# Summing six conditioning columns of layer 1 behind layer 0's last projections

## The chip, the cores and the metric

The kernel runs on one core of one Trainium2 chip. The metric is device time in microseconds (us), the median of three executions. TensorE (PE), VectorE (DVE), ScalarE (ACT) and GpSimd (POOL) compute; SyncE (SP) issues nearly all DMAs, one after the other in the order in which the code emits them.

## The reference

A trunk of two layers over 512 tokens of 1024 features, all in float32. A conditioning vector `c` gives six vectors of 1024 per layer, that is twelve columns of 512; each column is a product of the 1024 values of silu(c) with a 1024 x 512 block of `ada_w`.

```python
c_act = jax.nn.silu(c)
for i in range(DEPTH):                                   # DEPTH = 2
    mod = c_act @ ada_w[i] + ada_b[i]                    # 6 * 1024 = 12 columns of 512
    sh1, sc1, g1, sh2, sc2, g2 = jnp.split(mod[:, None, :], 6, axis=-1)
    h = x * (1 + sc1) + sh1
    y = neighbourhood_mixer(...) if i == 0 else gqa_mixer(...)
    x = layer_norm(DEEPNORM_ALPHA * x + (1 + g1) * y, ...)
    h = x * (1 + sc2) + sh2
    y = hierarchical_moe(h, ...)                         # 32 experts, each 6 MB of weights
    x = layer_norm(DEEPNORM_ALPHA * x + (1 + g2) * y, ...)
```

## The kernel before

**Stages.** Layer 0 has a neighbourhood attention (`mixer0`), then the output projection with the router (the loop over `sums`, `turnX`, `logits`), then the mixture of experts (`moe`, 16 pairs of experts). Layer 1 is the same with another attention.

**The loop around the change.** `flow` (line 155) writes out the order of layer 0's attention by hand, for PE, DVE and SP. It has 32 steps n, one for each pair of heads i = n // 4 and query block b = n % 4. A step emits: the scores of step n+1, some projection matmuls (`fill`), `close` of the finished pair of heads, the transposes of the probabilities (`turn`), a DVE share of one conditioning column (`adav`), `aside`, more projection matmuls, `adap` where the table `ADAP` names the step, and the weighted sum of the values (`weigh`). The projections of `STREAM` supply `fill`; they read the normalised input `hTH`, `hTL` and run out by step 27. Then `end` (the function `done`) closes the pool `ht0` that holds the input, opens in its memory four tiles `wh` for the split of the output weights `wo`, and from step 28 on `aside` calls `step`, which splits one quarter of `wo` into two parts.

**Conditioning columns.** Layer 0's columns 0 to 3 come first. Seven columns (`ADAV`) are summed on DVE. The others (`ADAP`, line 47) are summed on PE in `adap` (line 689): a column has eight products of a 128 x 32 slice of `Z` with a 128 x 512 slice of the weights, in four column groups of the array, so two of eight go to each group; the sum stands in a PSUM tile `pt` and DVE adds it to `mod[l]` (line 699). Layer 1's columns 6 to 11 are taken in pairs at steps 15, 19 and 23, its column 3 alone at step 26.

**Weights.** `plan` lists all loads in the order of their use, and `W` (line 242) issues them on SP as slots of `wp` (five tiles of 1 MB), and later of other pools, come free. A column needs two loads of 1 MB. SP holds strictly to its order: a load whose slot is still being read holds all that are behind it. The last loads of the attention are column (1, 3) and the four of `wo`; the third and fourth of `wo` take the two slots that column (1, 3) leaves.

**After the loop.** `close(7)` scales the last heads, `flush` adds the last DVE column. Then `layer` opens on the same side of the memory the pools `hr` and `wk`: `g1` (two `row` matmuls into `pw`, line 934, and line 935), and `oH`, `oL` (lines 1019, 1020), the split of the attention's output, which the first output projection (`pw<-w,oH`) reads. Tiles of a new pool wait for the last reader of the tiles whose memory they take.

Of the kernel before, what the change touches and what calls it, by code (L numbers as in the profile page):

```python
# [8 lines left out]
F32 = mybir.dt.float32  # L9
# [4 lines left out]
OP = mybir.AluOpType  # L14
# [3 lines left out]
P = 128  # L18
# [7 lines left out]
F = 512  # L26
# [17 lines left out]
QPOST = 2  # L44
NWQ = 4
ADAV = [(0, 6), (0, 7), (0, 8), (0, 9), (1, 0), (1, 1), (1, 2)]
ADAP = {4: [(0, 4), (0, 5)], 8: [(0, 10), (0, 11)], 12: [(1, 4), (1, 5)], 15: [(1, 6), (1, 7)], 19: [(1, 8), (1, 9)],
        23: [(1, 10), (1, 11)], 26: [(1, 3)]}
STREAM = [("qk", 1, 0)] + [("qk", n, i) for i in (1, 2) for n in range(2)] + [("vq", 0)] \
    + [("qk", n, i) for i in (3, 4, 5, 6) for n in range(2)] + [("vq", 1)] + [("qk", n, 7) for n in range(2)]  # L50
RATE = (18, 15)
# [10 lines left out]
def bcast(ap, shape):  # L62
    return ap.to_broadcast(shape)


class Trunk:
    def __init__(self, ctx, tc, a, out, dbg=None):
        self.ctx, self.tc, self.nc, self.a, self.out = ctx, tc, tc.nc, a, out
        self.dbg = dbg or {}
        self.wl = []  # L70
        self.qfree = NWQ
        self.wi = 0
        self.wt = {}
        self.wpos = {}
        self.extra, self.free, self.owed, self.nh = [], [0] * NWB, 0, None

# [5 lines left out]
    def plan(self):  # L82
        a, wl = self.a, self.wl

        def add(key, ap, dst=None):
            self.wpos[key] = len(wl)
            wl.append((key, ap, dst))

        def ada(l, *js):
            for j in js:  # L90
                for h in range(2):
                    add(("ada", l, j, h), a["ada"][l, j, h])

        def direct(key, ap, dst):
            add(key, ap, dst)

        def xs(c0, c1):
            for t in range(NT):
                direct(("x", t, c0), a["x"][t][:, c0:c1], self.X[t][:, c0:c1])

        def aq(j, c):
            add(("aq", j, c), a["adaq"][j, c])

        for n, t in self.early:
            direct(n, a[n], t)
        for g in range(4):
            aq(g // 2, g % 2)
            aq(2 + g // 2, g % 2)
            if g == 0:
                for l in range(DEPTH):  # L110
                    direct(("adab", l), a["adab"][l], self.mod[l][0:NR])
                xs(0, 256)
                add(("v", 0, 0), a["wv"][0])
                add(("qk", 0, 0), a["wqk"][0, 0])
            elif g == 1:
                xs(256, 512)
            elif g == 2:
                xs(512, 1024)
                add(("v", 0, 1), a["wv"][1])
        for n, t in self.late:  # L120
            direct(n, bcast(a[n], [P, 36]) if n[:2] == "rb" else a[n], t)
        def ask(z):
            if z[0] == "ada":
                add(z, a["ada"][z[1], z[2], z[3]])
            elif z[0] == "qk":
                add(z, a["wqk"][z[1], z[2]])
            else:
                add(z, a["wvq"][z[1]])

        none = lambda *n: None  # L130
        self.flow(ask, lambda z, ahead: chunk_dry(z, ahead), none, none, none, none, lambda z, h, k: k or ask(("ada", *z, h)),
                  lambda pair: [ask(("ada", *z, h)) for z in pair for h in range(2)], none, none)
        for l in range(DEPTH):
            if l:
                for c in range(2):
                    add(("kv", c), a["wkv1"][c])
                for c in range(4):
                    add(("q1", c), a["wq1"][c])
            for h in range(2):
                for kh in range(2):  # L140
                    add(("wo", l, h, kh), a["wo"][l, h, kh])
            for h in range(2):
                for kh in range(2):
                    add(("wl", l, h, kh), None)
            for j in range(E // 2):
                for n in range(2):
                    for kh in range(2):
                        for i in range(2):
                            add(("gu", l, 2 * j + i, n, kh), a["gu"][l, 2 * j + i, n, kh])
                for fh in range(2):  # L150
                    for i in range(2):
                        add(("dn", l, 2 * j + i, fh), a["dn"][l, 2 * j + i, fh])
            self.wend = getattr(self, "wend", []) + [len(wl)]

    def flow(self, split, chunk, scores, turn, weigh, close, adav, adap, aside, end):


        todo, made, ready = list(STREAM), [0], set()

        def ahead():  # L160
            if todo:
                z = todo.pop(0)
                split(z)
                ready.add(z)

        def stream():
            for z in STREAM:
                if z not in ready:
                    ahead()
                for _ in chunk(z, ahead):  # L170
                    made[0] += 1
                    yield
            while True:
                made[0] += 1
                yield

        it, due, n = stream(), {}, 0
        for z in STREAM:
            n += 48 if z[0] == "vq" else 24
            due[z] = n  # L180

        def fill(n):
            for _ in range(n):
                next(it)

        def need(z):
            fill(max(0, due[z] - made[0]))

        need(("qk", 1, 0))
        scores(0)  # L190
        for n in range(32):
            i, b = n // 4, n % 4
            if n + 1 < 32:
                if b == 3:
                    need(("qk", 1, i + 1))
                scores(n + 1)
            rate = RATE[n >= 12]
            fill(rate // 2)
            if b == 0 and i:
                close(i - 1)  # L200
            turn(n)
            if i < len(ADAV):
                for k in range(2):
                    adav(ADAV[i], b // 2, 2 * (b % 2) + k)
            aside(n)
            fill(rate - rate // 2)
            if n in ADAP:
                adap(ADAP[n])
            if n == 16:
                need(("vq", 0))  # L210
            if n == 24:
                need(("vq", 1))
            weigh(n)
            if n == 27:
                end()
# [137 lines left out]
    def ada_cols(self, pool, mod, dst, js, tag):  # L353
# [4 lines left out]
        for n, j, one in js:  # L358
            nc.vector.tensor_scalar(dst[:, n].rearrange("p (j i) -> p j i", j=2),
                                    pc[:, :, j:j + 2].rearrange("p i j -> p j i"), one, None, op0=OP.add)  # L360

    def row(self, ps, l, j):
        return self.mm(ps, bcast(self.indc[:, j:j + 1], [P, P]), self.mod[l], True, True)

# [64 lines left out]
    def mixer0(self, oT, right):  # L429
        tc = self.tc  # L430
        with tc.tile_pool(reuse_waits="tile", name="v0", bufs=1) as vp:
            self.qk_pool = vp
            V = vp.tile([P, NT, D], F32, name="V")
            V6 = vp.tile([P, NT - 1, D], F32, name="V6")
            ht = tc.tile_pool(reuse_waits="tile", name="ht0", bufs=1, side="right")
            hp = ht.__enter__()
            hH = hp.tile([P, KD, S], F32R, name="hTH")
            hL = hp.tile([P, KD, S], F32R, name="hTL")
            self.qpool = hp
            wo = []  # L440
            with tc.manual_schedule(engines={mybir.EngineType.PE, mybir.EngineType.DVE}), \
                    tc.tile_pool(reuse_waits="tile", name="n0p", bufs=2, space=PSUM) as pp:
                q0 = self.values(vp, pp, hp, hH, hL, V, V6)
                with tc.tile_pool(reuse_waits="tile", name="n0", bufs=1) as pool:
                    def done():
                        ht.__exit__(None, None, None)
                        wo.extend(self.split_wo(0, right("wh", 4)))

                    self.neighbours(pool, pp, hp, hH, hL, V, V6, oT, q0, done, lambda: wo[1]())
        return wo  # L450

    def split_wo(self, l, pool):
# [133 lines left out]
    def neighbours(self, pool, pp, hp, hH, hL, V, V6, oT, q0, done, step):  # L586
        nc, a = self.nc, self.a
# [41 lines left out]
        bias, pr, pt, po, rz = {}, {}, {}, {}, {}  # L629
# [40 lines left out]
        def close(i):  # L670
            self.scaled(pool, pp, oT[i // 4][:, i % 4, :].rearrange("p (b q) -> p b q", b=4), po[i], rz[i])
# [17 lines left out]
        def adap(pair):  # L689
# [8 lines left out]
                                tile_position=(0, r))  # L698
            nc.vector.tensor_tensor(self.mod[l], self.mod[l], ps, op=OP.add)

        def aside(n):
            i, b = n // 4, n % 4
            if b == 1 and i and i % 2 == 0:
# [6 lines left out]
            if n >= 28:  # L710
                step()

        self.flow(split, chunk, scores, turn, weigh, close, adav, adap, aside, done)
        close(7)
        self.accs, self.accl = [(j, accs.pop((l, j))) for l, j in ADAV[6:]], 1
        self.flush(pp)

# [919 lines left out]
```

## Time and profile before

| | |
|---|---|
| median of 3 runs | 1659.25 us (1657.05 to 1659.85) |
| the profiled execution | 1659.12 us; span from first to last instruction 1657.4 us |
| busy: PE, DVE, ACT, POOL | 95%, 42%, 26%, 10% of the span |
| layer 0's attention loop | 71 to 288 us |
| layer 0's output projection and router | 292 to 372 us |
| layer 0's experts | 377 to 850 us |
| DMA | 493 MB, 298 GB/s over the span, 419 GB/s beside the experts |

Times in the views are microseconds from the span's start. "Idle before" names what ended an engine's wait; SPq is SP's sequencer; PEclk is the granted clock of TensorE, 1.00 for 2.4 GHz and 0.50 for 1.2 GHz. A float32 product is two matmul instructions, so a column's eight products are 16 instructions.

### The profile page before, as it was taken

The numbers are of one execution on the slowest core, as the hardware profiler recorded it, in microseconds if no ns is written. First come the engines' busy times: TensorE is split into PE (matmuls) and PEld (weight loads), VectorE is DVE, ScalarE is ACT, GpSimd is POOL, SyncE is SP. The second block draws the span as 40 slices with busy tenths as digits, with TensorE's granted clock in tenths as the row PEclk, the third lists the DMA queues.
The fourth block names the chain that finished last, engine by engine and source line by source line (L and its number), as shares of the span: only waits on it lengthen the run. The fifth ranks groups of instructions, "written<-read, shape, count | busy, mean of one in ns | idle before, by whom it ended". The sixth has DMA issues, their size and how long they took to land. (4 is left out here: it accounts for less than half of the span.)

```text
span 1657.4 us, 21364 instructions
## 1 busy us (share of the span) xinstructions
PE 1569.4 (95%) x8490; PEld 903.9 (55%) x8490; DVE 700.5 (42%) x1605; ACT 437.8 (26%) x934; POOL 162.7 (10%) x99
## 2 busy tenths in 40 slices
PE   7999997989999999999989989998999999999995
PEld 5676664673544545455448866766444545445442
DVE  3434545574332322323256865666432322323235
ACT  2343335231110111111134475453111111101112
POOL 2322212010000000000013250011000000000001
PEclk9999997999999999999989999999999999999997
DMA  9586972358999999999942000035999999999971
GB/s 335 185 314 261 353 290 105 152 203 328 413 419 420 419 419 420 419 419 420 419 154 83 27 1 26 1 127 206 418 412 420 420 419 420 419 420 419 419 326 52
DMA packets 76198, 493.17 MB, mean 298 GB/s; under 512 B 9876, under 2 KB 11284, under 8 KB 18876
## 3 DMA queue, kind: packets, MB, share of 16 engines
q1 hardware_dynamic: 72636, 485.44, 72.1%
q10 hardware_dynamic: 3456, 6.29, 1.2%
q8 instruction: 69, 1.13, 0.3%
q14 instruction: 37, 0.30, 0.1%
HBM read 489.61 MB, written 2.10 MB: 297 GB/s over the span
## 5 line engine op out<-in xcount | busy, mean ns | idle before, releaser
L300 PE MATMUL gu<-w,xT 128*64 128x512 f32 x2048 | 445.1, 592 | 0.0
L300 PEld LDWEIGHTS gu<-w,xT 128*64 128x64 f32 x2048 | 146.8, 137 | 291.8 <-issue 285.5
L300 PE MATMUL pd<-w,hx 128*64 128x512 f32 x1024 | 226.8, 595 | 0.0
L1391 DVE TENSOR_TENSOR h<-h,gu 128x512 f32<-128x512 f32 x32 | 22.0, 688 | 367.5 <-PE gu L300 367.5
L300 PEld LDWEIGHTS pd<-w,hx 128*64 128x64 f32 x1024 | 70.7, 137 | 137.9 <-issue 134.3
L300 PE MATMUL gc<-OH,zH 128*128 128x256 f32 x480 | 121.8, 291 | 2.4 <-DVE OH L1276 2.4
L300 PE MATMUL gc<-OH,zL 128*128 128x256 f32 x480 | 118.9, 285 | 0.0
L300 PE MATMUL gc<-YH,OT 128*128 128x512 f32 x244 | 104.1, 427 | 1.0 <-DVE X L1358 1.0
L1358 DVE TENSOR_TENSOR X<-X,gc 128x512 f32<-128x512 f32 x128 | 87.3, 687 | 39.5 <-PE gc L300 39.5
L313 POOL TENSOR_TENSOR wl<-w,wh 128x1024 fp32r<-128x1024 f32 x19 | 46.1, 2431 | 559.5 <-DMA kk<-in_gain 494.4
L300 PEld LDWEIGHTS gc<-OH,zH 128*128 128x128 f32 x480 | 92.7, 193 | 14.7 <-issue 11.4
L300 PE MATMUL gc<-YL,OT 128*128 128x512 f32 x244 | 96.3, 395 | 0.0
L300 PEld LDWEIGHTS gc<-OH,zL 128*128 128x128 f32 x480 | 92.9, 193 | 0.0
L300 PE MATMUL pw<-w,oH 128*128 128x512 f32 x256 | 87.5, 413 | 0.4 <-DVE g L935 0.4
L1294 ACT ACTIVATE xT<-gc,A 128x256 f32<-128x256 f32 x60 | 33.8, 566 | 174.1 <-PE gc L300 174.1
L1414 ACT ACTIVATE YH<-h 128x512 fp32r<-128x512 f32 x32 | 20.2, 630 | 219.8 <-DVE h L1413 219.8
L300 PE MATMUL pj<-wh,hTH 128*128 128x256 f32 (+1 forms) x272 | 70.9, 303 | 6.7 <-ACT wh L312 2.8
L300 PE MATMUL pj<-wl,hTH 128*128 128x256 f32 (+1 forms) x272 | 68.0, 292 | 0.0
L300 PE MATMUL pj<-wh,hTL 128*128 128x256 f32 (+1 forms) x272 | 65.3, 292 | 1.4 <-DVE hTL L427 1.4
L300 PEld LDWEIGHTS gc<-YH,OT 128*128 128x128 f32 x244 | 45.8, 188 | 37.2 <-DVE X L1358 15.7
L1390 ACT ACTIVATE h<-gu 128x512 f32<-128x512 f32 x32 | 19.1, 597 | 174.3 <-PE gu L300 174.3
L1292 DVE TENSOR_SCALAR xT<-gc,A 128x256 f32<-128x256 f32 x60 | 32.5, 544 | 76.7 <-ACT xT L1294 76.3
(345 smaller groups left out, 2362.9 us busy)
## 6 DMA issues: line engine op xcount, KB each, us to landing
w<-in_gu SPq DMA_DIRECT2D x256, 1024.0 KB, 13.9
w<-in_dn SPq DMA_DIRECT2D x128, 1024.0 KB, 13.2
w<-in_ada SPq DMA_DIRECT2D x40, 1024.0 KB, 7.6
wq<-in_wqk SPq DMA_DIRECT2D x16, 512.0 KB, 3.6
w<-in_wo SPq DMA_DIRECT2D x8, 1024.0 KB, 4.8
w<-in_adaq SPq DMA_DIRECT2D x6, 1024.0 KB, 11.5
bias<-in_nab ACTq DMA_DIRECT2D x24, 256.0 KB, 4.4
w<-in_wq SPq DMA_DIRECT2D x4, 1024.0 KB, 4.8
```

The costliest lines, as they stand in the source:

```text
L300: return self.nc.tensor.matmul(out, l, r, start=start, stop=stop, **kw)
L313: (eng or nc.gpsimd).tensor_tensor(lo, src, h.bitcast(F32), op=OP.subtract)
L1292: nc.vector.tensor_scalar(xT[q][:, k, :], ps, s, b, op0=OP.mult, op1=OP.add)
L1294: nc.scalar.activation(xT[q][:, k, :], ps, AF.Identity, scale=s, bias=b)
L1358: nc.vector.tensor_tensor(X[t][:, c], X[t][:, c], ps, op=OP.add)
L1390: nc.scalar.activation(h, gu[0], AF.Silu)
L1391: nc.vector.tensor_tensor(h, h, gu[1], op=OP.mult)
L1414: nc.scalar.activation(YH[j][:, c], y, AF.Copy)
```

## The change

Layer 1's columns 6 to 11 leave the table `ADAP` and the list of `plan`. A list `qa` of 24 loads of 512 KB takes their place, four for a column. `done` opens a pool `aq0` of four such tiles (2 MB, one column) right behind the `wh` tiles, in memory that the closed pool `ht0` held, and issues the first four loads behind `wo`'s. `adaq` sums one column: eight products that read the four tiles in turn, one DVE add, and then the next four loads, each of which waits on SP until its tile has been read. It is called at steps 28 to 31, between `aside` and `weigh`, and twice behind `close(7)`. The pool is closed before the pools `hr` and `wk` are opened, which so take its memory.

```diff
-ADAP = {4: [(0, 4), (0, 5)], 8: [(0, 10), (0, 11)], 12: [(1, 4), (1, 5)], 15: [(1, 6), (1, 7)], 19: [(1, 8), (1, 9)],
-        23: [(1, 10), (1, 11)], 26: [(1, 3)]}
+ADAP = {4: [(0, 4), (0, 5)], 8: [(0, 10), (0, 11)], 12: [(1, 4), (1, 5)], 26: [(1, 3)]}
+ADAQ = [(1, j) for j in (8, 9, 6, 7, 10, 11)]
...
+        self.qt, self.qa = [], [(l, j, h, x) for l, j in ADAQ for h in range(2) for x in range(2)]
...
             if n in ADAP:
                 adap(ADAP[n])
+            if n > 27:
+                adaq()
...
+    def ada_tiles(self):
+
+        while self.qfree and self.qa:
+            l, j, h, x = z = self.qa.pop(0)
+            t = self.qpool.tile([P, 1024], F32, name="wa", bufs=NWQ)
+            self.nc.sync.dma_start(t, self.a["ada"][l, j, h][:, 1024 * x:1024 * x + 1024])
+            self.qt.append((z, t.rearrange("p (k n) -> p k n", k=2)))
+            self.qfree -= 1
...
                     def done():
                         ht.__exit__(None, None, None)
                         wo.extend(self.split_wo(0, right("wh", 4)))
-
-                    self.neighbours(pool, pp, hp, hH, hL, V, V6, oT, q0, done, lambda: wo[1]())
+                        self.qpool = qp.enter_context(tc.tile_pool(reuse_waits="tile", name="aq0", bufs=1, side="right"))
+                        self.ada_tiles()
+
+                    with ExitStack() as qp:
+                        self.neighbours(pool, pp, hp, hH, hL, V, V6, oT, q0, done, lambda: wo[1]())
...
+        def adaq():
+            if self.qt:
+                l, j = self.qt[0][0][:2]
+                ps = pp.tile([P, F], F32, name="pt")
+                for n in range(4):
+                    _, w = self.qt.pop(0)
+                    self.qfree += 1
+                    for k in range(2):
+                        kk = 2 * n + k
+                        r = 32 * (kk % 4)
+                        self.mm(ps[r:r + 32], self.Z[:, kk, 12 - j:44 - j], w[:, k, :], kk < 4, kk > 3, tile_position=(0, r))
+                nc.vector.tensor_tensor(self.mod[l], self.mod[l], ps, op=OP.add)
+                self.ada_tiles()
...
         close(7)
+        adaq()
+        adaq()
```

## Rows read from the trace of the kernel before

**Rows 1.** Page, part 1: busy time, share of the span, instructions.

```profile
PE 1569.4 (95%) x8490; PEld 903.9 (55%) x8490; DVE 700.5 (42%) x1605; ACT 437.8 (26%) x934; POOL 162.7 (10%) x99
```

**Rows 2.** Table by stretch: busy of each engine, granted clock, DMA share, GB/s.

```profile
core 0: us, PE busy (x) PEld busy (x) DVE busy (x) ACT busy (x) POOL busy (x), PEclk, DMA share, GB/s
150.00:200.00 50.00, 48.56 (x305) 31.26 (x304) 26.68 (x54) 19.25 (x45) 11.95 (x5) 1.00 0.90 352
250.00:300.00 50.00, 40.58 (x209) 24.56 (x208) 24.53 (x54) 22.02 (x54) 11.04 (x8) 0.76 0.41 153
500.00:800.00 300.00, 300.00 (x1544) 145.25 (x1542) 85.55 (x164) 41.38 (x81) 0.00 (x0) 1.00 1.01 419
```

**Rows 3.** Waits, 380 to 845: PE's for DMAs; us in total, times, longest.

```profile
PEld gu L300 <- DMA w<-in_dn: 2.0, 7, 0.3
PEld pd L300 <- DMA w<-in_gu: 0.9, 3, 0.3
```

**Rows 4.** Timeline of PE: the summed columns at steps 15, 19, 23 and 26.

```profile
177.80 2.78 PE L300 MATMUL pt<-w,Z 128*32 128x512 f32 x24
182.02 1.06 PE L300 MATMUL pt<-w,Z 128*32 128x512 f32 x8 [1.44 <-DMA w<-in_ada]
...
205.89 3.64 PE L300 MATMUL pt<-w,Z 128*32 128x512 f32 x32
...
237.98 3.64 PE L300 MATMUL pt<-w,Z 128*32 128x512 f32 x32
...
263.01 3.64 PE L300 MATMUL pt<-w,Z 128*32 128x512 f32 x16
```

**Rows 5.** Timeline of PE, 229 to 295: waits and the way into the output projection.

```profile
231.74 0.80 PE L300 MATMUL pj<-hTH,wh 128*128 128x512 f32 x1 [2.46 <-ACT V L479]
...
274.06 0.63 PE L303 MATMUL pt<-c_ident,rze 128*128 128x128 f32 x4 [2.27 <-DVE rze L886]
...
276.19 1.12 PE L300 MATMUL po<-pts,V 128*64 128x128 f32 x8 [1.07 <-DVE w L893]
...
288.02 1.12 PE L300 MATMUL po<-pts,V 128*64 128x128 f32 x8 [0.75 <-ACT pts L658]
...
290.19 1.92 PE L300 MATMUL pt<-dacc,Zo 128*32 128x512 f32 x2
292.04 2.19 PE L300 MATMUL pw<-mod,c_indc 128*128 128x512 f32 x4
294.68 0.73 PE L300 MATMUL pw<-w,oH 128*128 128x512 f32 x2 [0.45 <-DVE g L935]
```

**Rows 6.** Timeline of SP, and time to landing of each: `wo`'s third and fourth load.

```profile
265.00 0.33 SPq L272 DMA_DIRECT2D w<-in_wo  x1
...
DMA to landing us min/median/max: 4.8/4.8/4.8
...
266.71 0.33 SPq L272 DMA_DIRECT2D w<-in_wo  x1
...
DMA to landing us min/median/max: 6.8/6.8/6.8
```

**Rows 7.** Page, part 6: loads of 512 KB; count, size, median us to landing.

```profile
wq<-in_wqk SPq DMA_DIRECT2D x16, 512.0 KB, 3.6
```

**Rows 8.** Table by stretch, cut where the granted clock changes; columns as in rows 2.

```profile
231.05:237.90 6.85, 6.16 (x16) 4.57 (x16) 2.00 (x4) 2.36 (x6) 0.00 (x0) 0.50 0.44 157
...
261.80:268.60 6.80, 6.80 (x35) 2.96 (x34) 0.69 (x1) 3.51 (x8) 0.00 (x0) 0.50 0.36 125
268.60:275.40 6.80, 3.14 (x26) 1.99 (x24) 5.10 (x15) 4.91 (x14) 2.69 (x2) 1.00 0.49 184
275.40:292.50 17.10, 13.25 (x59) 7.42 (x60) 11.45 (x21) 8.19 (x20) 8.35 (x6) 0.50 0.14 42
```

**Rows 9.** Timelines of ACT and DVE: split of the attention's output, and `g1`.

```profile
265.49 1.14 ACT L1019 ACTIVATE oH<-w 128x512 fp32r<-128x512 f32 x2
...
293.96 1.27 DVE L935 TENSOR_SCALAR g<-pw 128x512 f32<-128x512 f32 x2
```

**Rows 10.** DVE's adds of a column sum: count, ns min/median/max, first and last start.

```profile
L699 DVE TENSOR_TENSOR mod<-mod,pt x7: 687/690/690, 103.1 to 266.7; 128x512 f32<-128x512 f32 x7
```

More of the change, by code (lines that the diff above doesn't have):

```diff
@@ L131, in plan @@
         self.flow(ask, lambda z, ahead: chunk_dry(z, ahead), none, none, none, none, lambda z, h, k: k or ask(("ada", *z, h)),
-                  lambda pair: [ask(("ada", *z, h)) for z in pair for h in range(2)], none, none)
+                  lambda pair: [ask(("ada", *z, h)) for z in pair for h in range(2)], none, none, none)
         for l in range(DEPTH):
@@ L153, in plan, with flow @@
             self.wend = getattr(self, "wend", []) + [len(wl)]
-    def flow(self, split, chunk, scores, turn, weigh, close, adav, adap, aside, end):
+    def flow(self, split, chunk, scores, turn, weigh, close, adav, adap, adaq, aside, end):
         todo, made, ready = list(STREAM), [0], set()
@@ L711, in aside @@
                 step()
-        self.flow(split, chunk, scores, turn, weigh, close, adav, adap, aside, done)
+        self.flow(split, chunk, scores, turn, weigh, close, adav, adap, adaq, aside, done)
         close(7)
+        adaq()
+        adaq()
+        assert not self.qa and not self.qt
         self.accs, self.accl = [(j, accs.pop((l, j))) for l, j in ADAV[6:]], 1
```

## The prediction

> **What bounds the kernel now.** I read the busy shares first: PE works 95% of the span, everything else less than half [rows 1]. Such a share is a mean over stages, so the table by stretch comes next [rows 2]. In the attention loop PE is at 48.6 of 50 us; from 250 to 300 it falls to 40.6 of 50 at a mean granted clock of 0.76; beside the experts it is at 300 of 300 with the DMAs at 419 GB/s. Both PE and DMA are full there, so the waits decide which of them leads: from 380 to 845 PE waits for weights ten times, 2.9 us in all, never over 0.3 us [rows 3]. The experts thus run at PE's pace, and a microsecond won or lost before 377 is one at the end. The change lies wholly before that. The question is therefore when the first matmul of the output projection starts, which is 294.68 [rows 5].
>
> I cut the time before it at a point both kernels have: T, the end of column (1, 3)'s sum at step 26, 263.01 + 3.64 = 266.65 [rows 4]. What is removed lies before T, what is added behind it.
>
> **Before T: three pairs of columns go.** They take 2.78 + 1.06 us with a wait of 1.44 us for their weights between them at step 15, then 3.64 us at step 19 and 3.64 us at step 23 [rows 4]: 12.56 us from start to end, some 0.2 us less as neighbouring matmuls overlap, so 12.4 us. PE is full in this stretch [rows 2] and in order, so the gain is taken whole: T moves to about 254.3. Nothing hides it and nothing else was hidden by it; the matmuls of `fill` and `turn` around them stay. Three DVE adds of 0.69 us [rows 10] also go, on an engine that waits there for PE. The loads behind them on SP (the projections' weights, `wo`'s first two) only come earlier. The bound below for this part is 12.4 - 3 us, if one more stretch at half clock falls into it, the one above 12.4 + 3 us: the wait of 2.46 us at step 22 to 23 (a PSUM buffer that ACT must empty) is followed by 6.85 us at clock 0.50 with 6.16 us of matmul work [rows 5, 8]. If the clock stays at 1.00 there, half of that work's time, 3.1 us, is won as well. The wait itself stays, so I take nothing.
>
> **Behind T: what PE must do.** Six columns are 96 matmul instructions. Sixteen take 3.64 us at clock 0.50, and 32 as long at 1.00 [rows 4, 8], so a column costs 1.8 us at full and 3.6 us at half clock. Steps 28 to 31 have room for some of it: they run from about 274 to 288 in a chain from engine to engine, PE waits 0.75 to 2.27 us in each (six waits from 268.7 on, of which three stand in [rows 5]), and the clock is at 0.50 with 13.25 of 17.10 us busy [rows 8]. With PE's work alone the six columns would nearly fit.
>
> **Behind T: what the loads must do.** They are the term that decides. SP keeps its order, so the new loads stand behind `wo`. The third and fourth loads of `wo` wait for the two slots of column (1, 3), at T - 1.65 and T + 0.06, and the fourth lands 6.8 us after its issue [rows 4, 6], T + 6.9. The first four tiles are issued right behind it and move in its wake: 2.10 MB at 419 GB/s [rows 2] are 5.0 us, T + 11.9. PE has come to step 28's call by about T + 7 (in the kernel before the transposes of that step end at 276.19 - 1.07 = 275.12, T + 8.5, behind a wait of 2.27 us for DVE [rows 5], of which I let 1.5 go, since DVE's early share of the split of the attention's output moves behind the columns), so it waits for tiles. The last tile's four instructions end the first column at T + 12.6.
>
> Every further column needs its own 2.10 MB, and there are only four tiles: a tile is asked for again when its products are through. Lower bound: the transfer never pauses, 5.0 us for a column. Upper bound: nothing overlaps; the first tile's load takes 3.6 us to land [rows 7], three more follow at 1.25 us each (512 KB at 419 GB/s), the last is read in 0.5 to 0.9 us, 8 us in all. Between them lies the nearest row, two loads issued 1.7 us apart: `wo`'s third lands 4.8 us after its issue and the fourth 3.7 us later [rows 6], where 1 MB at 419 GB/s would take 2.5 us. That is 283 GB/s with two in flight; with two to four in flight I take the middle, some 360 GB/s, so 5.8 us a column. Between two columns at steps 28 to 31 PE does `weigh`, scores and transposes in about 2 us at full clock (3.4 us at half, [rows 5]); their loads run meanwhile, so this lies beside the transfer. Five columns more: 29.0 us, and the last ends at T + 41.6.
>
> What queues behind these waits: PE is in order, so `weigh` of steps 28 to 31 and the scores behind it stand still with the column; DVE's add for it (0.69 us) stands ahead of the scores' maxima of the next step; on SP the first expert weights stand behind all 24 loads. The last of these is no cost: expert weights are wanted at 377, and SP is through by about T + 36.
>
> Then the way into the output projection. In the kernel before it is 294.68 - 290.19 = 4.5 us from `flush` to the first matmul, mostly at half clock [rows 5]. In the changed kernel one more DVE add stands in it, and the tiles of `hr` and `wk` (`oH` among them) take the memory of the four tiles, so the first splits of the attention's output, done at 265.49 in the kernel before [rows 9], must wait for the last column's products; against that, PE may be at full clock. Bounds 2.5 and 4.5 us, I take 3.5.
>
> **The sum.** New start of the output projection: T + 12.6 + 29.0 + 3.5 = T + 45.1. Before: 294.68 - 266.65 = T + 28.0. Loss 17.1 us, gain 12.4 us: slower by 4.7 us. The profiled execution took 1659.12 us (span 1657.4), 0.1 us under the median of 1659.25, so the forecast is 1664 us. With the bounds of the unknown terms: 5.0 us a column and 2.5 us at the end give T + 40.1, a change of -0.3 us, 1659; 7 us a column and 4.5 us at the end give T + 52.1, +11.7 us, 1671.
>
> **The rivals.** A measurement of this kernel can tell about 0.2%, 3.3 us, from no change.
>
> Same: the four tiles keep the DMA engines full, 5.0 to 5.3 us a column. For it: four loads in flight reach 419 GB/s beside the experts [rows 2]. Against it: there the loads don't wait for one another's readers. Result 1659 to 1661.
>
> Faster: the clock. Removing work shifts the wait at step 23 against the clock's changes, and columns on PE fill the idle steps. If the stretch at 231 keeps clock 1.00 (3.1 us) and the columns also come at 5.0 to 5.3 us, the result is 1659 - 3.1 to 4, about 1655.5. For it: in the steps before, waits of 1.44 us left the clock at 1.00 [rows 2, 4]. Against it: the wait of 2.46 us stays. It decides from the point where a column costs under 5.3 us, since above that the loss behind T eats the clock's gain.
>
> Clearly slower: PE stands at half clock through the six columns. Then `weigh`, scores and transposes (3.4 us) and a column's products (3.6 us) no longer fit beside the transfer, 7 us a column: 1671. For it: waits of about 1.1 us between short matmuls kept the clock at 0.50 from 275.40 to 292.50 [rows 5, 8], and the columns' waits for tiles will be as long. Against it: at 7 us PE would be busy without a gap, and the dense work at 261.80 to 268.60 ended with a return to 1.00 [rows 8].
>
> The Trainium skill ("TensorE: Matmul & The Clock Gate", section "Loop structure matters more than you think") names a wait for a DMA ahead of every group of matmuls as the loop that lets TensorE go cold, and that is how the moved columns are built: by that rule it is this last rival, 1671. The trace shows the fall to half clock behind one wait of 2.46 us and not behind one of 1.44 us [rows 4, 5, 8].
>
> **How the numbers follow.** Forecast (5.4 to 6.5 us a column) 0.42, same 0.28, faster 0.15, clearly slower 0.15. The forecast's own range reaches from 1661.5 to 1668, so a part of it (0.05) lies within 0.2%, and a part of the same rival (0.02) falls below it. Faster 0.17, same 0.31, slower 0.52. The range 1655 to 1671 takes in the faster and the clearly slower case at their centres and leaves out 0.2 beyond.
>
> **What the profile would show.** T at about 254. Twenty-four loads of 512 KB on SP, landing over some 36 us from about 255. Matmuls `pt<-w,Z` in six groups from about 262 to 296, with waits for `w<-in_ada` ahead of each; their spacing is the term to read: 5.0 is the same rival, 5.8 the forecast, 7 at clock 0.50 the slow one. First matmul of the output projection at about 299, and everything behind it shifted as a block. I am wrong if the spacing is 5 us or less, if T falls by much more or less than 12.4 us, or if the experts' pace changes.

## The result and the profile after

The changed kernel takes 1674.78 us (median of 4 runs, 1673.18 to 1675.61) against 1658.74 us of the kernel before on the same chip: a ratio of 1.0101, 95% interval 1.0088 to 1.0113. It is slower by 16 us, where 5 were forecast, and lies above the range. The profiled execution took 1675.56 us with a span of 1673.8, against 1659.12 and 1657.4 before.

The busy shares of the page hardly moved (they answer to [rows 1]):

```profile
PE 1579.0 (94%) x8490; PEld 905.7 (54%) x8490; DVE 695.9 (42%) x1608; ACT 437.5 (26%) x934; POOL 161.0 (10%) x99
```

The timeline of PE shows the whole loss. The columns are start, length, engine, line, operation, tiles, count, and in brackets the wait ahead of it with its releaser. The first line is column (1, 3), whose end is T; `wa` are the four new tiles; the last two lines answer to the last two of [rows 5].

```profile
250.08 3.64 PE L303 MATMUL pt<-w,Z 128*32 128x512 f32 x16
...
262.96 3.07 PE L303 MATMUL pt<-wa,Z 128*32 128x512 f32 x12
266.24 1.05 PE L303 MATMUL pt<-wa,Z 128*32 128x512 f32 x4 [0.21 <-DMA wa<-in_ada]
...
273.22 1.05 PE L303 MATMUL pt<-wa,Z 128*32 128x512 f32 x4 [1.42 <-DMA wa<-in_ada]
274.45 1.05 PE L303 MATMUL pt<-wa,Z 128*32 128x512 f32 x4 [0.18 <-DMA wa<-in_ada]
...
281.05 1.05 PE L303 MATMUL pt<-wa,Z 128*32 128x512 f32 x4 [0.22 <-DMA wa<-in_ada]
...
288.41 1.05 PE L303 MATMUL pt<-wa,Z 128*32 128x512 f32 x4 [0.19 <-DMA wa<-in_ada]
...
296.29 1.05 PE L303 MATMUL pt<-wa,Z 128*32 128x512 f32 x4 [0.21 <-DMA wa<-in_ada]
...
304.23 0.62 PE L303 MATMUL pt<-wa,Z 128*32 128x512 f32 x2 [2.19 <-DMA wa<-in_ada]
...
304.68 0.60 PE L303 MATMUL pt<-wa,Z 128*32 128x512 f32 x2
...
305.22 3.64 PE L303 MATMUL pw<-mod,c_indc 128*128 128x512 f32 x4
...
309.15 0.70 PE L303 MATMUL pw<-w,oH 128*128 128x512 f32 x2 [0.29 <-DVE g L967]
```

T is 250.08 + 3.64 = 253.72, 12.9 us earlier than before. The six columns end at 267.29, 275.5, 282.1, 289.46, 297.34 and 305.28: the first at T + 13.6, then five in 38.0 us, **7.6 us a column**. The output projection starts at 309.15 = T + 55.4, 14.5 us later than before. The first matmul of layer 0's experts goes from 376.74 to 392.19 (15.5 later) and layer 1's from 1154.81 to 1171.50 (16.7 later); the span grows by 16.4. So most of the loss is there when the output projection starts.

What PE waits for between 250 and 312 (total us, times, longest), and the table by stretch from the first column to the end of the last, and the 3.4 us behind it (columns as in [rows 2]):

```profile
PE pt L303 <- DMA wa<-in_ada: 11.2, 14, 2.2
PEld pt L303 <- DMA wa<-in_ada: 24.5, 17, 3.1
...
264.20:305.20 41.00, 28.48 (x152) 7.05 (x146) 10.37 (x23) 8.84 (x22) 7.48 (x6) 1.00 0.88 297
305.20:308.60 3.40, 3.40 (x7) 1.18 (x4) 3.27 (x6) 0.00 (x0) 0.00 (x0) 0.50 1.01 426
```

PE is at full clock for 41 us and idle for 12.5 of them. The DMA engines are at work for 0.88 of the time and move 297 GB/s (the first expert weights, from 297.76 on, included), where beside the experts they are at work all the time and move 419 [rows 2]. They are thus idle for only an eighth of the time; the rest of the missing rate is that they move less while at work. The loads themselves, from the instructions of line 370 and from SP's timeline (they answer to [rows 6, 7]):

```profile
L370 SPq DMA_DIRECT2D wa<-in_ada x24: 327/328/1154, 254.2 to 297.4; - x24
...
DMA to landing us min/median/max: 3.8/6.2/10.6
...
264.66 33.05 SPq L370 DMA_DIRECT2D wa<-in_ada  x20
...
297.76 0.42 SPq L275 DMA_DIRECT2D w<-in_gu  x1
```

Twenty of the 24 loads are asked for over 33 us, each when a tile's products are through. A load takes 6.2 us to land at the median, where the loads of `wq`, of the same size, took 3.6 [rows 7]. Reading a tile takes 1.05 us; at the median it starts 0.04 us after the landing, and the next load is issued 0.04 us after its end, with some delays of up to 0.6 us. I count 1.3 us for all of it, which is rounded up. A tile thus comes round every 6.2 + 1.3 = 7.5 us, and as a column needs each of the four tiles once, that is nearly the 7.6 us. The fourth tile of a column gives the exact sum: its five reloads took 7.1, 5.5, 6.2, 6.7 and 6.8 us to land, 6.5 on the mean, and with 1.05 and twice 0.04 us that is 7.6.

### The profile page after: what moved, and what is told of

Read it like the earlier page. It is cut to its first block, busy times and chain, and to the rows that moved or that the text cites. A ratio compares the mean times of both kernels' runs of the same rounds, so it can differ in the third digit from the quotient of the medians.

```text
span 1673.8 us, 21401 instructions
## 1 busy us (share of the span) xinstructions
PE 1579.0 (94%) x8490; PEld 905.7 (54%) x8490; DVE 695.9 (42%) x1608; ACT 437.5 (26%) x934; POOL 161.0 (10%) x99
## 5 line engine op out<-in xcount | busy, mean ns | idle before, releaser
L303 PE MATMUL pw<-w,oH 128*128 128x512 f32 x256 | 88.1, 416 | 0.3 <-DVE g L967 0.3
## 6 DMA issues: line engine op xcount, KB each, us to landing
w<-in_dn SPq DMA_DIRECT2D x128, 1024.0 KB, 12.9
```

The source lines that it names most:

```text
L303: return self.nc.tensor.matmul(out, l, r, start=start, stop=stop, **kw)
```

## The experiments

**Theory A**: too few bytes are under way; each tile waits for its reader and then for a long landing, and more tiles bring the pace to the bandwidth's 5.0 us. **Rivals**: the size of the packets (half rows of 4 KB) sets the landing (theory C); PE's order (the steps' other work between the columns) sets the pace (theory B); or the columns' own work on PE and DVE is the price and the loads lie beside it. Ratios are to the kernel before, timed on the same chip in the same series (its medians were 1657.07, 1658.54 and 1657.92 us); intervals are 95%.

**Eight tiles instead of four**, nothing else changed. The count of free tiles `qfree`, which starts at four, is replaced by one that starts at eight; the other versions with another number of tiles have the same edit, which is not shown there.

```diff
+        self.afree = 8
...
-            t = self.qpool.tile([P, 1024], F32, name="wa", bufs=NWQ)
+            t = self.qpool.tile([P, 1024], F32, name="wa", bufs=8)
...
```

> Eight tiles of 512 KB in place of four, the rest as in the change. Theory A (loads in flight): the changed kernel takes 7.6 us a column because only four loads of 512 KB are under way and each lands 5.4 to 7.1 us after its issue; with up to eight under way the pace falls to 5.0 to 5.5 us, the output projection starts at about 298 instead of 309 and the time is 1661 to 1665 us. Theory B (PE's order): the pace is set by PE, which reads the tiles only between weigh, scores and transposes, so more tiles change nothing, 1673 to 1676 us. Theory C (rows of 4 KB): the loads move at 280 to 300 GB/s because their rows are short, so again nothing, 1673 to 1676 us.

Measured: 1662.49 us, ratio 1.0029 (1.0020 to 1.0039). The first column ends at 267.02 and the sixth at 293.71, 5.3 us a column, and the output projection starts at T + 43.9. The DMA view of the stretch 264.5 to 290, first of the changed kernel, with packets, MB and GB/s, then the queue's packets, MB and share of the 16 engines' time, and then loads, KB and median us to landing:

```profile
DMA packets 2024, 7.35 MB, mean 288 GB/s; under 512 B 233, under 2 KB 233, under 8 KB 2022
...
q1 hardware_dynamic: 2022, 7.33, 88.1%
...
wa<-in_ada SPq DMA_DIRECT2D x16, 512.0 KB, 6.2
```

and with eight tiles:

```profile
DMA packets 2851, 10.41 MB, mean 408 GB/s; under 512 B 317, under 2 KB 317, under 8 KB 2848
...
q1 hardware_dynamic: 2848, 10.37, 102.0%
...
wa<-in_ada SPq DMA_DIRECT2D x15, 512.0 KB, 9.1
```

A load lands later, 9.1 us instead of 6.2, but twice as many are under way. Two thirds of the loss (10.6 of 16.0 us, each against its own before) go with the number of tiles alone. Theory A holds for this part, and the packets, which are of the same size here, don't set the limit.

**No reloads**: the four tiles are loaded once and all six columns read them, so 20 of the 24 loads are left out, five columns hold wrong sums, and layer 1 routes other tokens to its experts.

```diff
-                    _, w = self.qt.pop(0)
-                    self.qfree += 1
+                    w = self.qt[n][1]
...
-                self.ada_tiles()
```

> The four tiles are loaded once and all six columns are summed from them, so twenty loads are left out and five columns hold wrong sums; PE's and DVE's work stays. Theories A and C (the loads are the price): the first column ends at T + 13.6 us as in the change, the others fit into the steps at some 4 us each, the output projection starts at about T + 34, that is 288 us, and the time is about 1652 us, under the kernel before. Theory B (PE's order): the columns take nearly what they took, 1668 to 1675 us. Layer 1 routes other tokens to its experts, so its own time is not compared.

Measured: 1652.67 us, ratio 0.9971 (0.9961 to 0.9981). PE's timeline of it:

```profile
268.06 1.92 PE L304 MATMUL pt<-wa,Z 128*32 128x512 f32 x16
...
271.72 1.92 PE L304 MATMUL pt<-wa,Z 128*32 128x512 f32 x16
...
279.06 3.64 PE L304 MATMUL pt<-wa,Z 128*32 128x512 f32 x32
```

The first column still waits for its loads and ends at 266.32. Behind it a column takes 1.92 us, the wait ahead of each is gone, and columns come every 3.3 us with the steps' other work between them ((282.70 - 266.32) / 5). The output projection starts at 286.59, T (252.25) + 34.3, as the expectation of theories A and C has it. PE's order is thus not what sets 7.6 us; the loads are.

**Two large tiles instead of four**: 1 MB each, whole rows of 8 KB; the bytes in the tiles are the same.

```diff
-            t = self.qpool.tile([P, 1024], F32, name="wa", bufs=NWQ)
-            self.nc.sync.dma_start(t, self.a["ada"][l, j, h][:, 1024 * x:1024 * x + 1024])
+            t = self.qpool.tile([P, 2048], F32, name="wa", bufs=2)
+            self.nc.sync.dma_start(t, self.a["ada"][l, j, h])
...
```

> The same 2 MB of tiles and the same bytes, as two loads of 1 MB with rows of 8 KB in place of four of 512 KB with rows of 4 KB. Theory A: as many bytes are under way, so the pace stays at 7 to 8.5 us a column, 1672 to 1679 us. Theory C (short rows are slow): the pace falls towards 6 us, 1664 to 1668 us.

Measured: 1670.42 us, ratio 1.0077 (1.0057 to 1.0096); 6.6 us a column, a landing of 4.8 us, 319 GB/s. Whole rows are a little quicker, and the pace stays far from 5.0 us. The result lies between the two theories: the form of the load has a share, and the amount under way has the larger one.

**Four large tiles**: as before, with four of 1 MB, so that 4 MB can be under way in whole rows.

```diff
-            t = self.qpool.tile([P, 2048], F32, name="wa", bufs=2)
+            t = self.qpool.tile([P, 2048], F32, name="wa", bufs=4)
...
```

> Four tiles of 1 MB with rows of 8 KB, that is as many bytes under way as with eight tiles of 512 KB. If bytes under way set the pace, as there: 5 to 5.7 us a column, 1661 to 1664 us. If small loads cost more by themselves (two tiles of 1 MB ran at 6.6 us a column, four of 512 KB at 7.6 us), the pace goes to 5.0 us and the time to 1657 to 1661 us.

Measured: 1664.41 us, ratio 1.0036 (1.0024 to 1.0049). The DMA view of the same stretch:

```profile
DMA packets 1467, 10.71 MB, mean 420 GB/s; under 512 B 161, under 2 KB 161, under 8 KB 161
...
wa<-in_ada SPq DMA_DIRECT2D x8, 1024.0 KB, 8.5
```

The DMAs are full, a column costs 5.0 us, which both expectations allow, and the kernel is still slower than before, by a little more than either had it. The best pace that the bandwidth allows doesn't pay for the move.

**Six tiles** of 512 KB, to see the pace between four and eight.

```diff
-            t = self.qpool.tile([P, 1024], F32, name="wa", bufs=NWQ)
+            t = self.qpool.tile([P, 1024], F32, name="wa", bufs=6)
...
```

> Six tiles of 512 KB, between the four of the change (7.6 us a column, 288 GB/s) and eight (5 to 6 us, 408 GB/s). If the bytes under way set the pace, with a landing of 6 to 8 us: 5.7 to 6.4 us a column, some 350 GB/s, 1664 to 1669 us. If there is a step at two whole columns, since a column's first tile is asked for only when the column before has been emitted: as with four tiles, 1672 to 1676 us.

Measured: 1666.21 us, ratio 1.0042 (1.0025 to 1.0059); 5.7 us a column, 382 GB/s, a landing of 6.9 us, as expected where the bytes under way set the pace. Six tiles land hardly later than four: half as many bytes more under way move a third more.

**Unbroken blocks**: four tiles as in the change, but the weights of the six columns come from an array in which each load's 512 KB are one block; the landing place and the packets are the same.

```diff
-            self.nc.sync.dma_start(t, self.a["ada"][l, j, h][:, 1024 * x:1024 * x + 1024])
+            self.nc.sync.dma_start(t, self.a["adah"][j - 6, h, x])
```

> As the change, four tiles of 512 KB, but the weights lie in HBM so that each load is one unbroken block; before, each of its 128 rows was the half of a row of 8 KB. If reading half rows is what makes the loads slow (four of 512 KB move at 288 GB/s, two of 1 MB at 319), a load lands in under 5 us, the pace falls to 6 us and the time to 1664 to 1668 us. If it is the number and size of the loads under way, nothing changes: landing 6.2 us, 7.6 us a column, 1673 to 1676 us.

Measured: 1670.84 us, ratio 1.0078 (1.0062 to 1.0095); 6.9 us a column, a landing of 5.5 us, 307 GB/s. The time lies between the two expectations. Of the 2.6 us by which the landing is longer than 3.6, the jumps between half rows explain 0.7.

**The six columns left out altogether**, to see the part that is removed by itself; their sums are missing from the output.

```diff
-ADAQ = [(1, j) for j in (8, 9, 6, 7, 10, 11)]
+ADAQ = []
```

> The six columns are left out altogether, with their loads and adds; layer 1's columns 6 to 11 then hold the bias alone, so layer 1 routes other tokens to its experts and only the time up to layer 0's experts is read closely. This is the removed half of the change by itself. By the forecast's first term T comes at about 254 and everything behind it runs as in the kernel before: output projection at T + 28 = 282 us, layer 0's first expert matmul at 364 instead of 376.7, 12 to 13 us less at the end, 1644 to 1647 us. Rival, part of the gain was never there because something else paces the steps 15 to 26: T at 257 or later, 1648 to 1655 us.

Measured: 1647.18 us, ratio 0.9930 (0.9912 to 0.9947), so 11.4 us less. PE's timeline:

```profile
251.38 3.45 PE L303 MATMUL pt<-w,Z 128*32 128x512 f32 x16
...
282.85 0.73 PE L303 MATMUL pw<-w,oH 128*128 128x512 f32 x2
```

T is 254.83, 11.8 us earlier than before, and the output projection starts at T + 28.0, the very distance of the kernel before. The removed half is as the prediction had it, within 0.6 us in the profile and 1.0 by the medians; the latter also hold a layer 1 that routes other tokens.

**Two columns moved instead of six**: columns 10 and 11 at steps 28 and 29, the others back at steps 15 and 19.

```diff
-ADAP = {4: [(0, 4), (0, 5)], 8: [(0, 10), (0, 11)], 12: [(1, 4), (1, 5)], 26: [(1, 3)]}
-ADAQ = [(1, j) for j in (8, 9, 6, 7, 10, 11)]
+ADAP = {..., 15: [(1, 6), (1, 7)], 19: [(1, 8), (1, 9)], 26: [(1, 3)]}
+ADAQ = [(1, j) for j in (10, 11)]
```

> Only layer 1's columns 10 and 11 are moved; the pairs of steps 15 and 19 stay where they were. T falls by 3.6 us alone. Theory A: the two columns end at T + 13.6 + 7.6 = T + 21 us, before the chain of steps 28 to 31 is over anyway, so they are hidden but for some 2 us, and the time is 1656 to 1659 us. Rival, a price by the column (16 us over six columns, 2.7 us each): 1664 us.

Measured: 1660.74 us, ratio 1.0020 (1.0008 to 1.0033). Both expectations missed it. PE's timeline:

```profile
261.01 3.64 PE L303 MATMUL pt<-w,Z 128*32 128x512 f32 x16
...
276.92 1.05 PE L303 MATMUL pt<-wa,Z 128*32 128x512 f32 x4 [0.22 <-DMA wa<-in_ada]
...
283.00 1.05 PE L303 MATMUL pt<-wa,Z 128*32 128x512 f32 x4 [1.06 <-DMA wa<-in_ada]
...
293.23 1.08 PE L306 MATMUL pt<-c_ident,rze 128*128 128x128 f32 x4 [2.52 <-DVE rze L918]
...
298.95 1.25 PE L303 MATMUL pw<-w,oH 128*128 128x512 f32 x2
```

The columns stand in PE's queue ahead of the steps' own work and wait for tiles there; at 293.23 PE then waits 2.52 us for DVE. The output projection starts at T + 34.3, so two columns cost 6.3 us behind T, and they bring about 2 us ahead of it (T is 264.65 instead of 266.65). The profiled execution took 1665.80 us, 5 over the median.

**The same two columns later**: eight tiles, all eight loads asked for at once, the products at steps 30 and 31.

```diff
-            if n > 27:
+            if n > 29:
...
-            t = self.qpool.tile([P, 1024], F32, name="wa", bufs=NWQ)
+            t = self.qpool.tile([P, 1024], F32, name="wa", bufs=8)
```

> As the kernel with two moved columns, but with eight tiles, so that both columns are loaded at once, and called at steps 30 and 31 in place of 28 and 29. Theory A: both have landed when they are called, they cost the 1 us or so each that does not fit into PE's waits, against 3.6 us won ahead of T: 1654 to 1657 us. Rival, what cost time with two columns at steps 28 and 29 was not the wait for tiles but the matmuls and the adds in the chain of steps 28 to 31: 1659 to 1662 us as there.

Measured: 1657.57 us against 1658.54, ratio 0.9992 (0.9983 to 1.0002): no difference, 0.6 us above what theory A allowed and below the rival.

```profile
280.28 3.35 PE L304 MATMUL pt<-wa,Z 128*32 128x512 f32 x16
...
284.73 1.92 PE L304 MATMUL pt<-wa,Z 128*32 128x512 f32 x16
...
293.20 0.73 PE L304 MATMUL pw<-w,oH 128*128 128x512 f32 x2 [0.61 <-DVE g L968]
```

No wait for a DMA stands ahead of the columns any more, and the output projection starts at 293.20, T (263.33) + 29.9: two columns cost 1.9 us instead of 6.3. Columns whose weights have landed fit almost whole into the idle time of the last steps. Two things were changed together, the number of tiles and the steps; what each gives by itself wasn't tried.

**Four columns moved**: 8 to 11, eight tiles, at steps 29 to 31 and one behind the loop; the pair of step 15 stays.

```diff
-ADAQ = [(1, j) for j in (8, 9, 6, 7, 10, 11)]
+ADAQ = [(1, j) for j in (8, 9, 10, 11)]
...
-            if n > 27:
+            if n > 28:
...
```

> Eight tiles, four columns (8 to 11; columns 6 and 7 stay at step 15), called at steps 29, 30, 31 and once behind close(7). Theory A (loads in flight, and a first call that comes before its tiles): the tiles of the first two columns have landed by T + 17 us, before step 30, and the others land about as they are asked for, so the four columns cost 2 to 3 us behind T against 7.2 us won ahead of it: 1651 to 1655 us, under the kernel before. Rival, a price by the column wherever it stands (2.7 us each, 10.8 us): 1659 to 1662 us.

Measured: 1658.12 us, ratio 0.9997 (0.9987 to 1.0007), the expectation of theory A missed by 3 us and the rival's by 1. T is 258.02, 8.6 us earlier, and the output projection starts at T + 34.9, 6.9 us more: the last two columns need a second round of loads and wait for it. Eight tiles hold two columns; the gain ends there.

**The pair with the wait moved**: as in the version of two later columns, but those of step 15, (1, 6) and (1, 7), where PE waited 1.44 us for weights [rows 4].

```diff
+ADAP = {..., 19: [(1, 8), (1, 9)], 23: [(1, 10), (1, 11)], 26: [(1, 3)]}
+ADAQ = [(1, j) for j in (6, 7)]
...
-            if n > 27:
+            if n > 29:
...
```

> As the kernel with two moved columns at steps 30 and 31 and eight tiles, but the pair that moves is that of step 15 (columns 6 and 7) in place of that of step 23. Its removal takes 5.3 us of PE's time away ahead of T, its wait of 1.44 us for weights included, in place of 3.6 us. If that wait goes with the pair, the time is 1654 to 1656 us, under the kernel before; if the wait passes on to the next load (the DMA queue is full from 150 to 200 us), it is 1656 to 1658 us, as with the pair of step 23.

Measured: 1655.64 us against 1657.92, ratio 0.9985 (0.9975 to 0.9995), the fastest of all that compute everything.

```profile
257.26 3.29 PE L304 MATMUL pt<-w,Z 128*32 128x512 f32 x16
...
279.68 1.92 PE L304 MATMUL pt<-wa,Z 128*32 128x512 f32 x16
...
289.23 0.73 PE L304 MATMUL pw<-w,oH 128*128 128x512 f32 x2 [0.61 <-DVE g L968]
```

T is 260.55, 6.1 us earlier, and the output projection starts at T + 28.7, so the pair costs 0.7 us behind T. In the profile 5.4 us are won at the output projection and at the experts (371.31), and the median gains only 2.3. The difference lies in the executions that were profiled: this one was the kernel's quickest, 1652.39, 3.3 us under its median, and the one of the kernel before, 1659.12, lies 1.2 over the median of this series. One profile tells T only roughly: in the eight kernels here that do the same work ahead of T (the change, those with other tiles or blocks, without reloads, without the columns) it lies between 252.25 and 256.19.

The paces side by side. The account is (landing + 1.3 us for reading and asking again) x (tiles that a column needs / tiles there are):

| tiles | landing, us | GB/s | account, us a column | measured |
|---|---|---|---|---|
| 4 of 512 KB (the change) | 6.2 | 288 | 7.5 | 7.6 |
| the same, unbroken blocks | 5.5 | 307 | 6.8 | 6.9 |
| 2 of 1 MB | 4.8 | 319 | 6.1 | 6.6 |
| 6 of 512 KB | 6.9 | 382 | 5.5 | 5.7 |
| 8 of 512 KB | 9.1 | 408 | 5.2 | 5.3 |
| 4 of 1 MB | 8.5 | 420 | 4.9 | 5.0 |
| no reloads | | | | 3.3 |

The landing is each run's own, so the table shows that a tile's round holds little besides landing and reading; it doesn't tell what sets the landing, which grows with the number of tiles. Two tiles of 1 MB are 0.5 us off: PE's clock fell there, and three of the twelve readings took 1.78 to 1.94 us where most took 1.07, together 2.4 us or 0.5 a column.

By the medians the change of 16.0 us divides into -11.4 for what is removed, +7.0 for the six columns' work behind T (no reloads against left out: -4.4 + 11.4) and +20.4 for the reloads. As layer 1 routes other tokens in both kernels that were left incomplete, the way from T to the output projection, which lies ahead of that, is the safer measure: 28.0 us without the columns, 34.3 without reloads and 55.4 with them, so +6.3 for the work and +21.1 for the reloads.

## Why the prediction was wrong, point by point

- **T earlier by 12.4 us**: measured 12.9 in the profile; the kernel without the columns has 11.8 in its profile and 11.4 by the medians. Right.
- **The first column at T + 12.6**: T + 13.6, 1.0 us late. The four tiles come in `wo`'s wake as described.
- **5.8 us for every further column: the step that failed.** It measured 7.6, which is 9.0 of the 10.3 us between the forecast T + 45.1 and T + 55.4. The sum took `wo`'s pair, 283 GB/s with two loads in flight [rows 6], as a value that would rise towards 419 with four, and chose the middle, 360. Four tiles of half the size moved 2.10 MB in 7.6 us, 276 GB/s. The step took the count of loads for what sets the rate; the runs show that it is the bytes that can be under way, 2 MB here (two of 1 MB gave 6.6 us, four of 512 KB 7.6, eight of 512 KB 5.3, four of 1 MB 5.0). That the pair's 283 is so near to 276 is in part luck, for it was read wrongly: the 3.7 us behind it run from the third load's landing to the fourth's, when the fourth alone was under way. The kernel before moves 312 GB/s with both under way and 268 with the one (columns as in [rows 2]):

```profile
266.70:269.80 3.10, 2.68 (x16) 1.53 (x16) 1.66 (x5) 0.44 (x2) 0.00 (x0) 0.69 0.81 312
269.80:273.50 3.70, 1.29 (x12) 0.72 (x12) 3.67 (x12) 3.10 (x11) 1.14 (x1) 1.00 0.68 268
```

- **The range.** The text gave 8 us as the upper bound of this term, and the range was made with 7. With 8 and its own 4.5 us for the end it would have been T + 57.1, 16.7 us slower, 1676, and would have held the time.
- **PE waits, not works, behind T**: right. Without the reloads the columns come every 3.3 us. The last column makes the same point inside the changed kernel: nothing else stands between it and the fifth, and it still took 7.9 us (297.34 to 305.28).
- **The end part of 3.5 us**: 3.9. The splits of the attention's output did move behind the columns, as argued from [rows 9]; PE's last wait is 0.29 us for DVE's `g` all the same:

```profile
301.04 2.17 ACT L1051 ACTIVATE oH<-w 128x512 fp32r<-128x512 f32 x4
```

- **The queue on SP**: the first expert weights were to go out at about T + 36 and went out at 297.76, T + 44, right behind the last tile. That tile took 6.8 us to land and PE waited 2.19 us for it, the longest wait of all; whether the expert weights took their share of the DMAs from it wasn't tried. Landings of 6.7 to 7.1 us stand in the middle of the ring too, with no expert weights under way.
- **The rivals.** "Same" was priced at 5.0 to 5.3 us a column. Four tiles of 1 MB reach 5.0 and the kernel is still 5.9 us slower than before, since there T is 256.19, only 10.5 us earlier, the first column ends at T + 14.2 and the end part takes 4.3; the lower end of the sum, -0.3 us, was too good even with the pace it assumed. "Clearly slower" has nearly the right time, by a mechanism that did not take place: it had PE at half clock, and PE was at 1.00 from 264.20 to 305.20. The rule of the Trainium skill that stands beside it ("TensorE: Matmul & The Clock Gate", section "Loop structure matters more than you think") speaks of a long wait for a DMA between every matmul. The prediction took it without the word "long". This loop has 14 waits of 0.2 to 2.2 us ahead of groups of 2 to 8 matmuls, and the trace shows no fall of the clock within it. Waits of that length do not rule it out, though: with two tiles of 1 MB, where they are 0.7 to 2.1 us ahead of groups of 8, the clock was at 0.50 from 284.6 to 288.1 and again through the end of the last column:

```profile
294.90:301.70 6.80, 5.47 (x19) 0.93 (x12) 1.65 (x3) 1.92 (x5) 0.00 (x0) 0.50 1.01 424
```

- **The experts' pace unchanged**: right for layer 0's. Of the span's 16.4 us, 14.5 are there at the start of the output projection, 1.0 comes between it and layer 0's experts, and some 1.2 more ahead of layer 1's (0.3 are won back at the end). In the first of these two places a stretch at half clock is 6.8 us long (339.30 to 346.10), where the kernel before has 3.4 us (326.60 to 330.00):

```profile
339.30:346.10 6.80, 5.69 (x15) 4.43 (x16) 2.72 (x18) 0.49 (x3) 0.00 (x0) 0.50 0.76 304
```

  Whether this is the cause wasn't tried.

What stays open is why up to 2 MB under way do not fill the DMAs, when 419 GB/s would move all four tiles in 5.0 us. The 3.6 us of the `wq` loads [rows 7] are a landing with little company: those issued at 68.8, 108.8 and 164.6 with nothing ahead of them took 3.4 to 3.5 us, and those at 95.9, 150.5 and 177.3, behind other loads, 7.0 to 10.4. The ring's shortest landing, 3.8 us, is that of its first reload, issued at 264.66 when only two loads were still to land. So part of the 6.2 us is sharing. Unbroken blocks take off 0.7 us. Why the engines, at work for 88% of the time, move less in it than with eight tiles was not found.

## What to carry to other kernels

For a ring of tiles that one reader empties, work out the time from one load of a tile to its next as landing plus reading, with a landing that the trace shows under the same company, and divide by the tiles; the bandwidth is only the floor. The company matters: loads of 512 KB landed in 3.6 us nearly alone, in 6.2 with four tiles and in 9.1 with eight. Before work is moved behind another stage, ask whether its weights can all be there by then: two columns with their own tiles went into idle steps for 0.7 to 1.9 us, two that waited for tiles in PE's queue cost 6.3. And where one unknown term has two bounds, the range is made with both of them.

## What the runs showed of the hardware

- The bytes that can be under way set the rate, and 2 MB were not enough: 288 GB/s with four loads of 512 KB, 319 with two of 1 MB, 382 with six of 512 KB, 408 with eight, 420 with four of 1 MB.
- The DMA share doesn't tell the rate: with four tiles the engines were at work for 88.1% of the time and moved 288 GB/s, with eight for 102.0% (the share of the traced packets can pass 100%) and moved 408. That is 71% of the rate at 86% of the share.
- The granted clock stayed at 1.00 for 41 us with PE busy for 28.48 of them, waits of up to 2.2 us included, where the work between them was columns of 512; with two tiles of 1 MB it fell to 0.50 at 284.6 and 294.9, behind waits of up to 2.1 us; before, with 13.25 of 17.10 us busy and mostly short matmuls, it stayed at 0.50 [rows 8].
